# Another order for the last gate/up tile's products in a two-FFN decoder step, new homes for four split weights, and a closing with priority

## The chip, the core and the metric

The kernel runs on one core of a Trainium2 chip. A core has a matrix engine (TensorE, "PE" in the profile; its weight loads are listed apart as "PEld"), a vector engine (VectorE, "DVE"), an activation engine (ScalarE, "ACT"), a general engine (GpSimd, "POOL") and a queue engine (SyncE, "SP") that only issues DMAs here. Each engine works through its own list of instructions, and semaphores tie the lists together. The metric is the device time of the program in microseconds, lower is better. The three runs of the kernel before took 1035.49, 1036.48 and 1035.54 us: median 1035.54.

## What is computed

One step of a hybrid decoder over 520 token columns (512 of a prompt and 8 single new tokens), model width 1024. The trunk is a half-step SwiGLU FFN, a mixer (pooling heads, and a state-space scan, beside each other), a second half-step FFN and a last normalisation:

```
def _swiglu(x, wg, wu, wd):
    return (jax.nn.silu(x @ wg) * (x @ wu)) @ wd
...
h = h + 0.5 * _swiglu(_rms_norm(h, ffn1_norm[l]), ffn1_w_gate[l], ffn1_w_up[l], ffn1_w_down[l])
m, p, c, s = _hybrid_mixer(_rms_norm(h, mix_norm[l]), ...)
h = h + m
h = h + 0.5 * _swiglu(_rms_norm(h, ffn2_norm[l]), ffn2_w_gate[l], ffn2_w_up[l], ffn2_w_down[l])
...
return _rms_norm(h, final_norm), ...
```

The FFN width is 2816. All data are float32. The change touches the ends of the two FFNs only.

## The kernel before

**Numbers in two parts.** A float32 operand is split into a high part (a cast to the reduced float32 that TensorE takes, on ACT) and a low part (the value less its high part, on DVE). A product of two such operands is three matmuls (`mm3`: high by high, high by low, low by high). `split` does this for a weight that lies in a raw buffer, `load_unit` loads the raw weight first.

**Gate and up by seven products.** The columns are held as two halves of 260. The FFN's 22 tiles of 128 rows need gate times x and up times x for both halves, and this is done in a Strassen-like scheme: instead of eight block products a tile takes seven, numbered 1 to 7, each of four `mm3`, 12 matmuls. `Ffn.load(f)` loads a tile's gate and up weights and makes four split pairs of them: `d1` (for products 1 and 2), `e1` (7 and 5), `e2` (6 and 3) and `d2` (4). `d1` and `d2` live in `wp`, tags `whi` and `wlo`, three buffers each; `e1` and `e2` live in the FFN's own pool `wx`, tags `shi` and `slo`, two buffers each. In the trace these are called by tile and letter: `whi_21a` is d1 of tile 21, `whi_21b` is d2, `shi_21c` is e1, `shi_21d` is e2.

`Ffn.product(f, p)` adds up into one of three accumulators in PSUM: products 1, 6, 7 and 4 one after another into `A`; 2 into the first half of `BE`; 5 and 3 into its second half. After 1, 6 and 7 ACT copies what `A` holds (`keep`), so the next product into `A` has to wait for the copy. `gates(f)` makes the gate from the finished `BE` and the copies. `close(f)` takes what product 4 leaves in `A`, multiplies it with the gate on DVE, and splits the result `g` (high part on ACT, low part on DVE). `step(f)` runs one tile: product 1, then product 4 and the closing of the tile before, then 5, 6, 3, 7, 2 and `gates`.

**Down.** `rest` runs the tiles in three chunks of 8, 8 and 6, and after each multiplies the chunk's `g` with the down weights. For each of eight output blocks d there is one unit of weights. In the last chunk a unit is 128 by 768: six k-steps, one for each tile, and the last of them needs `g` of tile 21. In FFN 1 the last chunk goes through `down`, with units from `load_unit`. In FFN 2 it goes through `down_by_half`, which does all eight blocks for the first half of the columns and then for the second. It begins with the first five k-steps of blocks 0 to 2 (15 matmuls each), which do not need tile 21. There, units 0 to 2 come from `load_unit`, into the three `whi`/`wlo` buffers; units 3 to 7 are split into `dhi` and `dlo` in the pool `hg` (called `wd` there), which is opened where the transformed input `xt` (tiles `xth`, `xtl`) lay. Every product reads `xt`, product 4 of tile 21 last, so nothing is written to `dhi` or `dlo` before that. Raw down weights come in pairs of buffers: units 0 and 1, 2 and 3, 4 and 5, 6 and 7 share a pair each, there are two pairs, and a pair is loaded again when both its units are split.

`done(d, b)` scales a finished block on DVE (`th`, line 406), adds it to `h` (line 407) and hands it on. The accumulators of `down_by_half` are the same PSUM banks: `BE` for blocks 0, 1, 4, 5 and `A` for 2, 3, 6, 7. A block can only start when the earlier one in its bank has been taken out by line 406.

**The order.** Tile lays out each engine's list when the kernel is built: it takes whatever its own simulated timeline says is ready, by priority, which normally is the order of the program. `tc.high_priority()` puts a block's instructions ahead of others that are ready. An engine's list is fixed from then on.

Of the kernel before, what the change touches and what calls it, by code (L numbers as in the profile page):

```python
# [10 lines left out]
F32R = mybir.dt.float32r  # L11
# [5 lines left out]
P = 128  # L17
# [6 lines left out]
KD = D // P  # L24
FFN = 2816
KF = FFN // P
# [35 lines left out]
def tile_trunk_step(ctx: ExitStack, tc: tile.TileContext, ins: dict, outs: dict):  # L62
# [7 lines left out]
    wp = ctx.enter_context(tc.tile_pool(name="wp", bufs=3, side="right"))  # L70
# [24 lines left out]
    def raw_tile(name):  # L95
        if not half:
            t = raw_pair(name)
            half.extend([t[:, 1], t[:, 0]])
        return half.pop()

    def split(src, n, name, hp, nb, tags):
        hi, lo = (hp.tile([P, 1024], F32R, tag=t, bufs=nb, name=f"{t}_{name}")[:, :n] for t in tags)
        h, l = hi, lo
        if len(src.shape) == 3:
            h, l = (t.rearrange("p (j c) -> p j c", j=src.shape[1]) for t in (hi, lo))
        nc.scalar.copy(h, src)  # L106
        nc.vector.tensor_tensor(out=l, in0=src, in1=h.bitcast(F32), op=ALU.subtract)
        return hi, lo

    def load_unit(src, n, name):  # L110
        raw = raw_tile(name)[:, :n]
        nc.sync.dma_start(out=raw, in_=src)
        return split(raw, n, name, wp, 3, ("whi", "wlo"))

    def mm3(ps, whi, wlo, xhi, xlo, start, stop, **kw):
        nc.tensor.matmul(ps, whi, xhi, start=start, stop=False, **kw)  # L116
        nc.tensor.matmul(ps, whi, xlo, start=False, stop=False, **kw)  # L117
        nc.tensor.matmul(ps, wlo, xhi, start=False, stop=stop, **kw)  # L118

    def ws(w, k, m=P):  # L120
        return w[:, k * m : (k + 1) * m]
# [73 lines left out]
    class Ffn:  # L195
# [111 lines left out]
        def rest(self, before, last_chunk):  # L307
            lo = 0
            for c, n in enumerate(CHUNKS):
                hi = lo + n  # L310
                last = hi == KF
                for f in range(self.direct if c == 0 else lo + 1, hi if last else hi + 1):
                    self.step(f)
                if last:
                    self.product(KF - 1, 4)
                    self.close(KF - 1)
                    wd = before()
                else:
                    self.product(hi + 1, 1)
                    self.product(hi, 4)  # L320
                    self.close(hi)
                if last and wd is not None:
                    self.down_by_half(c, lo, last_chunk, wd)
                else:
                    self.down(c, lo, hi, last_chunk if last else None)
                lo = hi

        def step(self, f):
            if f not in self.A:
                self.product(f, 1)  # L330
            if f - 1 not in self.g and f > self.direct:
                self.product(f - 1, 4)
                self.close(f - 1)
            for p in (5, 6, 3, 7, 2):
                self.product(f, p)
            self.gates(f)

# [39 lines left out]
        def down_by_half(self, c, lo, after, wd):  # L377
            n = KF - lo
            banks, units = {}, []
            for d in range(KD):  # L380
                src, name = ins[f"w{self.i}d"][d, :, lo * P :], f"{self.i}d{d}_{c}"
                if d < 3:
                    units.append(load_unit(src, n * P, name))
                    continue
                raw = raw_tile(name)[:, : n * P]
                nc.sync.dma_start(out=raw, in_=src)
                hi, lw = (wd.tile([P, n * P], F32R, tag=t, bufs=KD - 3, name=f"{t}_{name}") for t in ("dhi", "dlo"))
                nc.scalar.copy(hi, raw)
                nc.vector.tensor_tensor(out=lw, in0=raw, in1=hi.bitcast(F32), op=ALU.subtract)
                units.append((hi, lw))  # L390

            def part(d, b, ks):
                if (d, b) not in banks and d % 4 < 2:
                    t = ps[0].tile([P, 2, 512], F32, tag="BE", bufs=2, name=f"dh{self.i}_{d}{b}")
                    banks[d, b], banks[d + 1, b] = t[:, 0], t[:, 1]
                elif (d, b) not in banks:
                    banks[d, b] = ps[0].tile([P, 512], F32, tag="A", bufs=2, name=f"dh{self.i}_{d}{b}")
                wh, wl = units[d]
                for k in ks:
                    g = self.g[lo + k]  # L400
                    mm3(banks[d, b][:, :HB], ws(wh, k), ws(wl, k), g[:, 0, b], g[:, 1, b], k == 0, k == n - 1)

            def done(d, b):
                hs = HALVES[b]
                t = self.wx.tile([P, 2, HB], F32, tag="tg", bufs=2, name=f"th{self.i}_{d}{b}")[:, 0]
                nc.vector.tensor_tensor(out=t, in0=banks[d, b][:, :HB], in1=self.rn[:, hs], op=ALU.mult)
                nc.vector.tensor_tensor(out=h[:, d, hs], in0=t, in1=h[:, d, hs], op=ALU.add)
                after(d, b, hs)

            for d in range(3):  # L410
                part(d, 0, range(n - 1))
            for b in range(2):
                for d in range(KD):
                    part(d, b, range(n - 1, n) if b == 0 and d < 3 else range(n))
                    done(d, b)
# [629 lines left out]
```

## Time and profile before

| what | us |
|---|---|
| median of three runs | 1035.54 |
| the profiled execution, its own time | 1034.07 |
| its span (first to last instruction) | 1032.3 |
| PE busy in the span | 983.7 |
| end of FFN 1: last matmul of product 4 of tile 21 starts at | 338.49 |
| first matmul of the mixer starts at | 370.99 |
| end of FFN 2: last matmul of product 4 of tile 21 starts at | 980.34 |
| last down matmul of FFN 2 starts at | 1016.78 |

In the rows below, times are microseconds from the start of the span. A row of the timeline has start, duration, engine, line of the kernel, operation, output and inputs, shape and count; in brackets stands how long the engine had been idle before it and which instruction released it. "SPq" is the issue of a DMA. A matmul's shown duration (0.28) is longer than the distance from one start to the next (0.12), since they are pipelined: the distance is what it costs.

### The profile page before, as it was taken

How to read it: one execution, taken by the hardware profiler on the slowest of the kernel's cores; microseconds unless marked ns; L12 is line 12 of the kernel's file. 1: busy time of each engine (PE TensorE's matmuls, PEld its weight loads, DVE VectorE, ACT ScalarE, POOL GpSimd, SP SyncE). 2: the span in 40 equal slices, each digit the busy share in tenths (PEclk: the TensorE clock that was granted, in tenths of full speed). 3: DMA queues.
4: the chain of work that ended last, by engine and by line, in shares of the span. 5: the costliest groups of instructions: out<-in, count | busy, mean ns of one | idle time of the engine just before them, and what ended most of it. 6: DMA issues, size and time to landing. Idle time of an engine off the chain costs nothing.

```text
span 1032.3 us, 19314 instructions
## 1 busy us (share of the span) xinstructions
PE 983.7 (95%) x7848; PEld 958.9 (93%) x7848; DVE 809.1 (78%) x1403; ACT 526.4 (51%) x884; POOL 57.8 (6%) x109
## 2 busy tenths in 40 slices
PE   7999999999999999997798999999999999999984
PEld 6999999999999999997688999899999999999983
DVE  6999557995578787789989877999945899458766
ACT  7566314663145546775585435566622566225452
POOL 0000000000000001338211000000000000000000
PEclk9999999999999999998899999999999999999997
DMA  5333223232231233345444222223223232332213
GB/s 181 115 123 123 83 90 115 83 123 82 96 110 62 89 134 131 130 155 188 127 157 152 95 86 82 83 83 123 83 95 110 83 122 83 99 107 83 92 32 83
DMA packets 45352, 110.25 MB, mean 107 GB/s; under 512 B 5896, under 2 KB 17096, under 8 KB 45264
## 3 DMA queue, kind: packets, MB, share of 16 engines
q1 hardware_dynamic: 45264, 109.03, 31.9%
q8 instruction: 61, 1.00, 0.4%
q14 instruction: 27, 0.22, 0.1%
HBM read 101.67 MB, written 7.34 MB: 106 GB/s over the span
## 4 chain that ended last, share of the span: by engine, by line
PE 80%; DVE 9%; ACT 6%; issue 2%; DMA 2%; SPq 0%; DVEq 0%; ACTq 0%
PE A L116 7%; PE A L117 7%; PE A L118 7%; PE dn L118 7%; PE dn L116 7%; PE dn L117 7%; PE BE L116 6%; PE BE L118 5%; PE BE L117 5%; PE P L228 3%; PE wo L116 2%; PE wo L118 2%; PE wo L117 2%; PE inz L116 1%; PE inz L117 1%
## 5 line engine op out<-in xcount | busy, mean ns | idle before, releaser
L355 DVE TENSOR_TENSOR td<-dn,rn 128x520 f32<-128x520 f32 x40 | 27.9, 699 | 113.2 <-PE dn L118 113.2
L116 PE MATMUL dn<-g,whi_1d 128*128 128x260 f32 x352 | 99.5, 283 | 1.7 <-ACT whi_1d L106 1.5
L117 PE MATMUL dn<-g,whi_1d 128*128 128x260 f32 x352 | 99.3, 282 | 0.0
L118 PE MATMUL dn<-g,wlo_1d 128*128 128x260 f32 x352 | 99.2, 283 | 0.0
L116 PE MATMUL dn<-g,whi_2d 128*128 128x260 f32 x256 | 72.5, 283 | 1.6 <-ACT whi_2d L106 1.6
L117 PE MATMUL dn<-g,whi_2d 128*128 128x260 f32 x256 | 72.4, 283 | 0.0
L118 PE MATMUL dn<-g,wlo_2d 128*128 128x260 f32 x256 | 72.3, 284 | 0.0
L116 PEld LDWEIGHTS dn<-g,whi_1d 128*128 128x128 f32 x352 | 66.2, 188 | 2.4 <-ACT whi_1d L106 2.0
L117 PEld LDWEIGHTS dn<-g,whi_1d 128*128 128x128 f32 x352 | 66.3, 188 | 0.0
L118 PEld LDWEIGHTS dn<-g,wlo_1d 128*128 128x128 f32 x352 | 66.2, 188 | 0.0
L284 ACT COPY ac<-A 128x260 f32<-128x260 f32 x123 | 45.9, 373 | 37.7 <-PE A L118 36.1
L106 ACT CAST whi_1d<-raw_1d 128x1024 fp32r<-128x1024 f32 (+1 forms) x24 | 23.4, 979 | 73.0 <-PE dn L117 63.0
L106 ACT CAST whi_2d<-raw_2d 128x1024 fp32r<-128x1024 f32 (+1 forms) x19 | 19.3, 1018 | 68.4 <-PE dn L117 59.3
L228 PE MATMUL P<-xg_f,raw 128*128 128x260 f32 x192 | 45.9, 397 | 5.7 <-DMA raw<-in_w1gu 5.7
L116 PEld LDWEIGHTS dn<-g,whi_2d 128*128 128x128 f32 x256 | 48.4, 189 | 2.0 <-ACT whi_2d L106 2.0
L256 DVE TENSOR_TENSOR s<-raw 128x1024 f32<-128x1024 f32 x41 | 50.0, 1219 | 0.0
L117 PEld LDWEIGHTS dn<-g,whi_2d 128*128 128x128 f32 x256 | 48.3, 189 | 0.0
L228 PEld LDWEIGHTS P<-xg_f,raw 128*128 128x128 f32 x192 | 37.4, 199 | 11.6 <-ACT sq_f L154 5.7
L118 PEld LDWEIGHTS dn<-g,wlo_2d 128*128 128x128 f32 x256 | 48.1, 189 | 0.0
L116 PE MATMUL inz<-xh_mx,whi_inz 128*128 128x260 f32 x128 | 37.7, 294 | 0.0
L116 PE MATMUL wo<-catg,whi_wo 128*128 128x260 f32 x128 | 37.5, 293 | 0.2 <-DVE h L869 0.2
L116 PE MATMUL inx<-xh_mx,whi_inx 128*128 128x260 f32 x128 | 37.4, 292 | 0.0
(1326 smaller groups left out, 3933.9 us busy)
## 6 DMA issues: line engine op xcount, KB each, us to landing
raw<-in_w2gu SPq DMA_DIRECT2D x44, 512.0 KB, 3.8
raw<-in_w1gu SPq DMA_DIRECT2D x42, 512.0 KB, 4.4
raw_1d<-in_w1d SPq DMA_DIRECT2D x16, 512.0 KB, 3.9
raw_2d<-in_w2d SPq DMA_DIRECT2D x16, 512.0 KB, 4.1
raw_wo<-in_w_out SPq DMA_DIRECT2D x12, 512.0 KB, 4.7
h<-in_state_ssm SPq DMA_DIRECT2D x16, 256.0 KB, 4.4
ab<-scr_acs SPq DMA_DIRECT2D x8, 512.0 KB, 5.1
out_nss<-h SPq DMA_DIRECT2D x16, 256.0 KB, 3.0
```

The source lines that it names most:

```text
L106: nc.scalar.copy(h, src)
L116: nc.tensor.matmul(ps, whi, xhi, start=start, stop=False, **kw)
L117: nc.tensor.matmul(ps, whi, xlo, start=False, stop=False, **kw)
L118: nc.tensor.matmul(ps, wlo, xhi, start=False, stop=stop, **kw)
L228: nc.tensor.matmul(self.banks[f, u][b][:, :HB], ws(self.raw[f][:, u], j + 4 * q), xg[:, slot[q]], start=j == q == 0, stop=j == 3 and q == ...
L256: nc.vector.tensor_tensor(out=s1, in0=diag, in1=up0, op=ALU.add)
L284: nc.scalar.copy(keep, out[:, :HB])
L355: nc.vector.tensor_tensor(out=t, in0=banks[d][:, :, :HB], in1=self.rn.rearrange("p (b t) -> p b t", b=2), op=ALU.mult)
```

## The change

Three edits. In `rest`, the closing of the last tile gets priority, in both FFNs. In `step`, the last tile takes its products in the order 2, 5, 6, 3, 7 rather than 5, 6, 3, 7, 2, in both FFNs. In `down_by_half` (FFN 2), units 2 and 3 are now split into the `shi`/`slo` buffers that e1 and e2 of the tile leave; units 0 and 1 stay in `whi`/`wlo`, and 4 to 7 stay in the pool `hg`, with four buffers each rather than five. All units now go through `split` or the same two lines as before, with the DMA issued ahead of it.

```diff
                 if last:
                     self.product(KF - 1, 4)
-                    self.close(KF - 1)
+                    with tc.high_priority():
+                        self.close(KF - 1)
                     wd = before()
...
-            for p in (5, 6, 3, 7, 2):
+            for p in (2, 5, 6, 3, 7) if f == KF - 1 else (5, 6, 3, 7, 2):
                 self.product(f, p)
             self.gates(f)
...
             for d in range(KD):
                 src, name = ins[f"w{self.i}d"][d, :, lo * P :], f"{self.i}d{d}_{c}"
-                if d < 3:
-                    units.append(load_unit(src, n * P, name))
-                    continue
                 raw = raw_tile(name)[:, : n * P]
                 nc.sync.dma_start(out=raw, in_=src)
-                hi, lw = (wd.tile([P, n * P], F32R, tag=t, bufs=KD - 3, name=f"{t}_{name}") for t in ("dhi", "dlo"))
+                if d < 4:
+                    home = (wp, 3, ("whi", "wlo")) if d < 2 else (self.wx, 2, ("shi", "slo"))
+                    units.append(split(raw, n * P, name, *home))
+                    continue
+                hi, lw = (wd.tile([P, n * P], F32R, tag=t, bufs=KD - 4, name=f"{t}_{name}") for t in ("dhi", "dlo"))
                 nc.scalar.copy(hi, raw)
                 nc.vector.tensor_tensor(out=lw, in0=raw, in1=hi.bitcast(F32), op=ALU.subtract)
                 units.append((hi, lw))
```

## The prediction

> **What bounds the kernel now.** I read the page first, then PE's waits, then the two stretches that the change touches, FFN 1's end (312 to 376 us) and FFN 2's end (960 to 1033 us), engine by engine.
>
> ```profile
> span 1032.3 us, 19314 instructions
> PE 983.7 (95%) x7848; PEld 958.9 (93%) x7848; DVE 809.1 (78%) x1403; ACT 526.4 (51%) x884; POOL 57.8 (6%) x109
> ...
> PE 80%; DVE 9%; ACT 6%; issue 2%; DMA 2%; SPq 0%; DVEq 0%; ACTq 0%
> ```
>
> PE's list sets the time: 95% busy, and 80% of the chain that ended last. The change adds and removes no matmul, so it can only win or lose stops of PE. Its waits in FFN 2's last stretch (960 to 1033 us), as total, times, longest:
>
> ```profile
> PE psl L523 <- DVE acc_last L147: 2.9, 1, 2.9
> PE dh L116 <- DVE th L406: 2.7, 3, 1.5
> PE dh L116 <- ACT whi_2d L106: 0.8, 1, 0.8
> ```
>
> The first belongs to the last normalisation, behind the last down matmul, and stays. The other two are in what is edited (of the three times in the second row, two are shown below with 1.52 and 0.52; the third, 0.7, is at 1012, in the finish of the first half of the columns, and stays too). PE's own timeline shows what they cost:
>
> ```profile
> 979.04 0.28 PE L116 MATMUL A<-xth_f,whi_21b 128*128 128x260 f32 x1
> ...
> 980.34 0.28 PE L118 MATMUL A<-xth_f,wlo_21b 128*128 128x260 f32 x1
> 981.42 0.39 PE L116 MATMUL dh<-g,whi_2d 128*128 128x260 f32 x1 [0.80 <-ACT whi_2d L106]
> 981.65 0.28 PE L117 MATMUL dh<-g,whi_2d 128*128 128x260 f32 x1
> 982.16 0.38 PE L116 MATMUL dh<-g,dhi_2d 128*128 128x260 f32 x1 [0.23 <-ACT dhi_2d L388]
> 982.38 0.28 PE L117 MATMUL dh<-g,dhi_2d 128*128 128x260 f32 x1
> 982.50 0.31 PE L118 MATMUL dh<-g,wlo_2d 128*128 128x260 f32 x1
> ...
> 988.77 0.28 PE L118 MATMUL dh<-g,dlo_2d 128*128 128x260 f32 x1
> 990.57 0.39 PE L116 MATMUL dh<-g,whi_2d 128*128 128x260 f32 x1 [1.52 <-DVE th L406]
> ...
> 991.72 0.39 PE L116 MATMUL dh<-g,whi_2d 128*128 128x260 f32 x1 [0.52 <-DVE th L406]
> 991.94 0.28 PE L117 MATMUL dh<-g,whi_2d 128*128 128x260 f32 x1
> 992.06 0.28 PE L118 MATMUL dh<-g,wlo_2d 128*128 128x260 f32 x1
> ```
>
> Product 4 of tile 21 is 12 matmuls with eleven steps from 979.04 to 980.34, 0.12 us each. That is the price of a matmul here. Stop 1: from 980.34 to 982.50 there are five steps, 0.60 us of work in 2.16, so 1.56 us are lost. Stop 2: from 988.77 to 992.06 there are six steps (990.57, .79, .92, 991.72, .94, 992.06), 0.72 us in 3.29, so 2.57 us are lost. Together **4.13 us**. Why, the chain of waits tells, in order of time:
>
> ```profile
> 980.54 0.84 ACT whi_2d L106
> ...
> 982.28 0.96 DVE dlo_2d L389
> ...
> 983.26 0.33 SPq L386
> ...
> 983.63 4.70 DMA raw_2d<-in_w2d
> ...
> 988.35 0.84 ACT dhi_2d L388
> ...
> 989.21 0.96 DVE dlo_2d L389
> 990.17 0.35 DVE th L406
> ```
>
> Product 4 ends; only then may unit 2 be split (its `whi` was d2's) and unit 3 (its `dhi` lies where `xt` lay). Stop 1 is PE waiting for these. When unit 3's low part is made, its raw pair is free, SP issues the loads of units 6 and 7, the second lands 4.70 us later, unit 7 is split, and only then DVE comes to the first `th`, which stood behind that split in its list. Stop 2 is PE waiting for that `th` to empty a bank. Both stops hang on one event, the splits of units 2 and 3 after product 4.
>
> **The change, part by part.**
>
> *The new homes.* Unit 2 and unit 3 now want the buffers of e1 and e2 of tile 21: e2 is done with product 3, e1 with product 7, both ahead of product 4. The work is the same (one cast of 0.84, one subtraction of 0.96 each), only earlier. Stop 1 goes, unless what comes after product 4 is too little to cover the closing (below). The loads of 6 and 7 go out when unit 3 is split. Product 7 ends a little before 977 (next part); with the copy of `A`, the cast, the subtraction that is 979.2 or so, against 983.26. With 0.37 for the issue, 4.70 to land, 0.84 and 0.96 unit 7 is whole near 986, and the first `th` right behind it. The bank that it empties is wanted by block 6, when PE is through the six blocks before it: 108 matmuls, some 40 of them ahead of product 4, so 68 x 0.12 = 8.2 us after it, near 990. Four us of slack: stop 2 goes. Moved DMAs: the loads of 4 and 5, 6 and 7, on a SP queue that carries nothing else from there to the output:
>
> ```profile
> 967.04 17.73 SPq L386 DMA_DIRECT2D raw_2d<-in_w2d  x5
> 1008.87 18.09 SPq L534 DMA_DIRECT2D out_y<-hg  x8
> ```
>
> Value: -4.13; bounds -4.13 and -1.56 (rival A).
>
> *The order of products.* The same 12 matmuls stand earlier, cost nothing in themselves, and free d1 one tile-product earlier for unit 1. But product 2 used to stand between 6 and 7, or 7 and 4, while ACT copies `A`. The list keeps such successors far apart:
>
> ```profile
> 971.22 0.28 PE L118 MATMUL A<-xth_f,slo_21d 128*128 128x260 f32 x1
> ...
> 974.22 0.28 PE L116 MATMUL A<-xth_f,shi_21c 128*128 128x260 f32 x1
> ...
> 975.54 0.29 PE L118 MATMUL A<-xth_f,slo_21c 128*128 128x260 f32 x1
> ```
>
> From 6's last to 7's first it is 3.0 us, from 7's last to 4's first (979.04) 3.5 us, though the copy after 7 is done early:
>
> ```profile
> 976.25 0.36 ACT L284 COPY ac<-A 128x260 f32<-128x260 f32 x1
> ```
>
> Between 7 and 4 it puts down matmuls that need no tile 21. The rows by line count them before product 4 (each of the three lines of `mm3` has ten, 30 in all):
>
> ```profile
> L116 PE MATMUL dh<-g,whi_2d x10: 278/282/287, 974.0 to 978.7; 128*128 128x260 f32 x10
> ```
>
> With product 2 gone forward, only 3 (12 matmuls, 1.4 us) is left for the distance between 6 and 7, and some 10 more down matmuls will fill it: product 4 ends 1.2 us later with 40 down matmuls done instead of 30. PE is busy all the while, so by itself this costs 0. If nothing were put there, PE would have the copy to wait for, 0.94 us after 7's last began (976.25 + 0.36 against 975.54, less a step), 1.0 us at most in each FFN: bound +2.0.
>
> *The cover for the closing.* What PE has after product 4 that needs no `g` of tile 21: blocks 0 to 3, five k-steps, 4 x 15 = 60, now that unit 3 is split early; less 40 is 20 matmuls, 2.4 us. What the closing takes, before:
>
> ```profile
> 338.49 0.29 PE L118 MATMUL A<-xth_f,wlo_21b 128*128 128x260 f32 x1
> 339.43 0.62 ACT L299 CAST g<-tg 128x520 fp32r<-128x520 f32 x1
> 340.43 0.69 DVE L300 TENSOR_TENSOR g<-tg,g 128x520 fp32r<-128x520 f32 x1
> 983.48 0.62 ACT L299 CAST g<-tg 128x520 fp32r<-128x520 f32 x1
> 984.88 0.70 DVE L300 TENSOR_TENSOR g<-tg,g 128x520 fp32r<-128x520 f32 x1
> ```
>
> In FFN 1 the last part of `g` is ready at 341.12, 2.6 us after product 4's last began; in FFN 2 at 985.58, 5.2 us, for four casts stood ahead of it on ACT and four subtractions on DVE. With priority these can't go first once `g`'s own is ready; one may slip in while DVE makes the product with the gate, as in FFN 1. I take FFN 1's 2.6 us for both: against 2.4 + 0.12 of cover, 0.1 to 0.3 us of a stop. What the priority pushes back on ACT and DVE are the splits of units 4 to 7, wanted when PE gets to block 4, 20 + 12 matmuls after product 4 (3.8 us); unit 4 needs 0.84 + 0.96 and the closing's 1.4 in between. That fits. Value +0.2; bounds 0 and +2.6 (no cover left).
>
> *FFN 1.* Units 0 and 1 have 60 such matmuls too, less 40 is 20: the same 2.4 us. Its one stop in the edited stretch is for a bank, not for `g`:
>
> ```profile
> 343.53 0.28 PE L118 MATMUL dn<-g,wlo_1d 128*128 128x260 f32 x1
> 344.00 0.39 PE L116 MATMUL dn<-g,whi_1d 128*128 128x260 f32 x1 [0.19 <-DVE td L355]
> ```
>
> From there to 370 us PE has no stop; the busy times (the first pair is the stretch and PE) show it, and DVE with 23.98 of 26 us:
>
> ```profile
> 344.00:370.00 26.00, 26.00 (x216) 25.89 (x216) 23.98 (x53) 15.37 (x34) 0.42 (x1) 1.00 0.31 96
> ```
>
> Unit 2's split there waits for product 4 as before and is now behind the closing, some 1 us later, but its first matmul is the one at 344.00, 3 us after. Value 0; bounds -0.35 (that stop) and +2.6 (no cover).
>
> **Sum.** -4.13 + 0.2 + 0 = -3.9 us. The profiled execution took 1034.07 (span 1032.3 and 1.8 around it), which becomes 1030.2. The median of the runs is 1.5 above it, so on their scale 1035.54 - 3.9 = **1031.6**. If the mechanism works, its own range is 1030.8 to 1033.2.
>
> **The rivals.** A. *Only stop 1 goes.* Unit 3's cast is late, behind the closing that now has priority: product 4 ends near 981.7, the cast and subtraction near 983.5, the loads land near 988.6, unit 7 is whole near 990.4, and if the list keeps the first `th` behind it, PE wanting the bank from 990 waits for 2 us all told. For it: in the list of before `th` stands behind unit 7's split, and a list can't be changed at run time. The Trainium skill (TensorE: Matmul & The Clock Gate, under Architectural detail) says the same of the engine, that VectorE takes its queue strictly in order; the chain above agrees, with `th` at 990.17 right after the subtraction at 989.21. Against it: product 7 frees the home some 4 us before product 4 ends, and ACT is idle from 976.61 to 980.54. Price: gain 1.9, time 1033.6. Chance 0.15.
>
> B. *It doesn't do what it says*: the list leaves the splits of 2 and 3 behind product 4 though their homes are free. Then the stops stay, 1035.5. Against it: unit 0 and 1 were split as soon as theirs were free. Chance 0.06.
>
> C. *The cover is spent* (slower). The place is PE's list between product 7 and the closing, in both FFNs: the builder, now with four ready units, puts nearly all 60 down matmuls ahead of product 4. Then PE stands for the whole closing. Each matmul above some 38 ahead of product 4 costs 0.12 in each FFN, 0.24 together; the 4.13 is eaten from 38 + 17 = 55 on. With all 60 in front it is 2 x 2.6 = 5.2 us against 4.13, and up to 2.6 more if FFN 2's closing stays as slow as it is now (5.2): 1036.6 to 1039.2. For it: the distances of 3.0 and 3.5 us are the builder's own, and the new order gives it less to put between. Against: the two distances need some 40 matmuls, not 55. Chance 0.16.
>
> D. *Another order further on.* All lists after tile 21 of FFN 1 are laid out anew, with DVE nearly full from 344 to 370, and the mixer behind it. For a price I take the first of those PE stops either way, 1 to 3 us on top of the forecast: 1028.6 to 1034.6. For: any shift of DVE's order there falls on a list with 2 us to spare in 26. Against: FFN 1 ends at PE's own pace in both. Chance 0.11, half of each sign.
>
> **The numbers.** The forecast has 0.52. About 0.2%, 2.1 us, is what a measurement of this kernel can tell from no change: faster is below 1033.5, slower above 1037.6. Faster: 0.52, half of A's 0.15 and most of D, 0.09: 0.69. Same: half of A, B, the slower end of D and 0.06 of C: 0.21. Slower: the rest of C: 0.10. The range runs from D's better part to C's lower part, 1029.3 to 1036.8; outside are most of C and D's ends, some 0.17.
>
> **What would show it.** Stop 1 right: no gap in PE's list after product 4 of tile 21 above 0.3 us, and `shi_2d` casts ahead of product 4's end. Stop 2 right: the last two loads of down weights issued near 979 rather than 983.26, the first `th` near 986, no gap before block 6. The order: some 40 down matmuls ahead of product 4, whose end moves to about 981.7. The closing: 2.6 us in both FFNs. FFN 1: the first mixer matmul within 0.5 us of 370.99. The forecast is wrong if the loads of 6 and 7 still go out after product 4, if a new gap opens between 7 and 4 or before the first matmul on tile 21, or if the mixer's length changes.

## The result, and the profile after

The changed kernel is faster. The four first runs have a median of 1030.51 us against 1036.0 of the kernel before, a ratio of 0.9948 with a 95% interval of 0.993 to 0.9965. Timed twice more, in the experiments below, it gave 0.996 (0.9946 to 0.9974) and 0.9972 (0.9961 to 0.9983). So the gain is 3 to 5 us; its profiled execution took 1030.91 us against 1034.07, 3.2 less. Its page:

```profile
span 1029.1 us, 19313 instructions
PE 981.7 (95%) x7848; PEld 956.6 (93%) x7848; DVE 807.3 (78%) x1403; ACT 526.4 (51%) x884; POOL 57.0 (6%) x109
```

PE's waits from 955 us on in the changed kernel (who waits for what, the total in us, how often, the longest):

```profile
PE psl L525 <- DVE acc_last L147: 2.9, 1, 2.9
PE dh L116 <- DVE th L408: 1.2, 2, 0.7
```

The waits on `whi` and `dhi` are gone, that on `th` has shrunk from 2.7 to 1.2 us. The timeline of PE in the changed kernel at the two places where it stopped before (start, length, then the instruction; in brackets the wait ahead of it):

```profile
980.72 0.28 PE L118 MATMUL A<-xth_f,wlo_21b 128*128 128x260 f32 x1
980.83 0.28 PE L118 MATMUL dh<-g,slo_2d 128*128 128x260 f32 x1
...
987.74 0.28 PE L118 MATMUL dh<-g,wlo_2d 128*128 128x260 f32 x1
988.54 0.39 PE L116 MATMUL dh<-g,whi_2d 128*128 128x260 f32 x1 [0.52 <-DVE th L408]
988.76 0.28 PE L117 MATMUL dh<-g,whi_2d 128*128 128x260 f32 x1
...
990.69 0.28 PE L118 MATMUL dh<-g,wlo_2d 128*128 128x260 f32 x1
990.81 0.28 PE L116 MATMUL dh<-g,dhi_2d 128*128 128x260 f32 x1
```

Product 4 ends and the next matmul starts 0.11 us later, with unit 2 in its new home (`slo`). Stop 1 (1.56 us) is gone. Stop 2 is 0.78 us (988.76 less 987.74, less two steps of 0.12) where it was 2.57.

Which matmul waits there? From 988.54 to 990.69 stand 18 in a row on `whi_2d` and `wlo_2d`. In the changed kernel these hold units 0 and 1 only, and both have had their 36 matmuls of the first half by 987.74. So PE goes from block 4 straight to block 0 of the second half, ahead of blocks 5 to 7, and not to block 6, as the prediction has it. (The rows show that it is block 0 or 1; by the order of the program it is 0.) That block takes the pair of banks which blocks 0 and 1 leave, so it waits for the `th` of block 1, whose last matmul is the one at 987.74. The rows of before, in the prediction, can be read in the same way: stop 2 was two waits. First 1.79 us were lost up to 990.92, in the three matmuls of a block's last k-step (by its bank, block 1's), behind the first `th`; then 0.78 us up to 991.94, ahead of block 0 of the second half. The new homes took the first away, all but 0.07 us, and left the second as it was.

What feeds stop 2, from the same kernel's timeline of SP, ACT and DVE, in order of time (for SP the length runs over the x issues of one line):

```profile
972.81 7.04 SPq L384 DMA_DIRECT2D raw_2d<-in_w2d  x4
...
975.65 0.84 ACT L106 CAST shi_2d<-raw_2d 128x768 fp32r<-128x768 f32 x1 [2.39 <-PE BE L117]
977.10 0.83 ACT L106 CAST shi_2d<-raw_2d 128x768 fp32r<-128x768 f32 x1 [0.61 <-PE A L117]
...
980.91 1.57 ACT L390 CAST dhi_2d<-raw_2d 128x768 fp32r<-128x768 f32 x2 [2.17 <-PE A L117]
982.39 0.62 ACT L299 CAST g<-tg 128x520 fp32r<-128x520 f32 x1
...
983.53 0.69 DVE L300 TENSOR_TENSOR g<-tg,g 128x520 fp32r<-128x520 f32 x1
984.14 1.82 DVE L391 TENSOR_TENSOR dlo_2d<-raw_2d,dhi_2d 128x768 fp32r<-128x768 f32 x2
986.91 0.43 DVE L408 TENSOR_TENSOR th<-dh,rn 128x260 f32<-128x260 f32 x1 [0.96 <-PE dh L118]
```

Units 2 and 3 are split as products 3 and 7 let go of their homes, 5 and 4 us before product 4 ends. The last two loads are out by 979.85 instead of 983.6 and later. DVE is through with unit 7 at 985.96 and then stands idle 0.96 us: the first `th` now waits for PE, not PE for DVE's list.

To compare kernels whose mixers differ from one execution to the next (last section), I use two lengths from PE's timeline: **stage 1** from the tenth-last matmul of product 1 of tile 21 in FFN 2 to the first sum of squares (`psl`), and **stage 2** from there to the second `psl`. All times in us:

| kernel | stage 1 | stage 2 | ratio of the runs (95% interval) |
|---|---|---|---|
| before | 965.57 to 1005.46: 39.89 | 14.49 | |
| changed | 965.69 to 1002.32: 36.63 | 14.53 | 0.9948 (0.993 to 0.9965) |
| changed, e1 | 963.64 to 1000.27: 36.63 | 14.54 | 0.996 (0.9946 to 0.9974) |
| changed, e9 | 966.70 to 1003.30: 36.60 | 14.54 | 0.9972 (0.9961 to 0.9983) |
| e2 homes alone | 964.06 to 1000.69: 36.63 | 14.54 | 0.9967 (0.9954 to 0.998) |
| e3 order alone | 966.67 to 1006.67: 40.00 | 14.54 | 1.0001 (0.999 to 1.0011) |
| e4 priority alone | 962.75 to 1002.59: 39.84 | 14.54 | 0.9996 (0.9986 to 1.0006) |
| e5 unit 3 late | 964.86 to 1004.46: 39.60 | 14.52 | 0.9981 (0.9968 to 0.9994) |
| e11 unit 3 late, again | 965.45 to 1003.32: 37.87 | 14.54 | one run |
| e6 closing really first | 967.99 to 1004.53: 36.54 | 14.48 | 0.9967 (0.9953 to 0.998) |
| e7 and last steps first | 967.07 to 1003.07: 36.00 | 13.30 | 0.9955 (0.9941 to 0.997) |
| e8 and finish later | 965.49 to 1001.49: 36.00 | 12.85 | 0.9953 (0.9937 to 0.9968) |
| e10, as e8 | 965.94 to 1001.93: 35.99 | 12.86 | 0.9956 (0.9942 to 0.997) |

The change is worth 3.26 us in stage 1 and nothing in stage 2. At the end of FFN 1 the first mixer matmul starts at 370.76 (370.99 before), 0.1 us earlier when the 0.15 by which the first down matmul (111.17 against 111.32) was ahead already is taken off.

### The profile page after: what moved, and what is told of

Its sections match the earlier page's. It is cut to its first block, busy times and chain, and to the rows that moved or that the text cites. A ratio compares the mean times of both kernels' runs of the same rounds, so it can differ in the third digit from the quotient of the medians.

```text
span 1029.1 us, 19313 instructions
## 1 busy us (share of the span) xinstructions
PE 981.7 (95%) x7848; PEld 956.6 (93%) x7848; DVE 807.3 (78%) x1403; ACT 526.4 (51%) x884; POOL 57.0 (6%) x109
## 4 chain that ended last, share of the span: by engine, by line
PE 42%; DVE 7%; ACT 4%; DMA 2%; issue 1%; POOL 1%; DVEq 0%; ACTq 0%; SPq 0%
PE A L116 4%; PE A L117 4%; PE A L118 4%; PE dn L118 3%; PE dn L116 3%; PE dn L117 3%; PE BE L116 3%; PE BE L118 3%; PE BE L117 3%; PE wo L116 2%; PE wo L118 2%; PE wo L117 2%; PE P L228 1%; PE dh L116 1%; DMA bcb<-scr_bc 1%
## 5 line engine op out<-in xcount | busy, mean ns | idle before, releaser
L118 PE MATMUL inz<-xh_mx,wlo_inz 128*128 128x260 f32 x128 | 36.9, 288 | 0.0
```

## The experiments

Four kernels (e2 to e5) take the change apart, two (e6, e7) ask what is left of stop 2 and why, and one (e8) builds on the answer. e1, e9, e10 and e11 run a kernel again.

**e1, the changed kernel again.**

> The changed kernel once more, timed in five rounds. Theory T (the whole gain is the two stops at the end of FFN 2, -3.3 us there in the profile, nothing elsewhere): ratio 0.9969, 0.996 to 0.998. Rival R (the first timing's 0.9948 is real, 2 us more come from an earlier stage, such as the mixer): ratio 0.994 to 0.9955, and a profile with a mixer some 2 us shorter.

0.996, at the edge of T's range; the 0.9969 that the profile's 3.3 us would give lies within its interval, and so does R's 0.9955. Stage 1 is 36.63 us to the last digit. The third timing, e9, is 0.9972, with R's range outside its interval. In the mixer every engine's list is row for row that of the kernel before, so R has no place to gain in; why the first timing came out 2 us lower is not shown, other than that the mixer's length varies by as much between executions of one program.

**e2, the homes alone.** The changed kernel less the other two edits:

```diff
-            for p in (2, 5, 6, 3, 7) if f == KF - 1 else (5, 6, 3, 7, 2):
+            for p in (5, 6, 3, 7, 2):
...
-                    with tc.high_priority():
-                        self.close(KF - 1)
+                    self.close(KF - 1)
```

> Units 2 and 3 in the homes of e1 and e2, but the old order of products and no priority. Theory T (the homes carry it: e2 is free after product 3 and e1 after product 7, in the old order too, 8 and 5 us before product 4 ends): both stops go as in the changed kernel, -2.8 to -3.6 us, the loads of units 6 and 7 near 979. Rival R (the new order is what frees the homes in time): the gain is at most stop 1, -1.6 us, and the loads go out after product 4 as before, near 983.

The timeline of SP in this run, and then PE's waits from 950 us on:

```profile
954.91 21.98 SPq L383 DMA_DIRECT2D raw_2d<-in_w2d  x8
```

```profile
PE dh L116 <- DVE th L407: 1.2, 2, 0.7
```

All eight loads are out by 976.89, 2.1 us before product 4's last matmul (978.96) starts. Stage 1 is 36.63, the same as with all three edits. T holds: the homes are the whole gain of the stage. In the old order too, e2 and e1 are done well before product 4.

**e3, the order alone.** The kernel before, with `(2, 5, 6, 3, 7)` for the last tile.

> Product 2 first in the last tile of both FFNs, units 2 and 3 where they were, no priority. Theory T (12 matmuls moved under a busy PE): -0.5 to +0.5 us, stop 1 (1.6) and stop 2 (2.6) both still there, FFN 1's end within 0.3 us. Rival R (the order matters by itself, through the earlier split of unit 1): at least 1.5 us faster. Rival C of the prediction (fewer matmuls between 6 and 7, so the cover is spent): at least 1 us slower, with a new stop before the first matmul that needs tile 21.

PE's waits from 950 us on in this run:

```profile
PE dh L116 <- DVE th L406: 2.8, 3, 1.6
PE dh L116 <- ACT whi_2d L106: 0.8, 1, 0.8
PE dh L116 <- ACT dhi_2d L388: 0.2, 1, 0.2
```

Both stops are there as before, stage 1 is 40.00 against 39.89, the ratio 1.0001. T holds, and rival C of the prediction has no sign here: 30 down matmuls stand ahead of product 4, as many as before, and no new stop.

**e4, the priority alone.** The kernel before, with the closing under `tc.high_priority()`.

> Priority for the closing of the last tile, nothing else. Every engine's list of instructions is, row for row, that of the kernel before. Theory T (so the priority does nothing at all): no difference, 0.9985 to 1.0015, which is then the scatter of a program against itself; the closing in FFN 2 still ends 5.2 us after product 4's last matmul begins. Rival R (the closing gets ahead, as the prediction had it): 2.6 us there.

The timeline of PE and DVE around the closing in this run:

```profile
977.52 0.28 PE L118 MATMUL A<-xth_f,wlo_21b 128*128 128x260 f32 x1
978.60 0.39 PE L116 MATMUL dh<-g,whi_2d 128*128 128x260 f32 x1 [0.80 <-ACT whi_2d L106]
...
982.06 0.69 DVE L300 TENSOR_TENSOR g<-tg,g 128x520 fp32r<-128x520 f32 x1
```

`g` is ready at 982.75, 5.2 us after product 4's last matmul, as before, and stop 1 is there. The ratio is 0.9996. The lists show why: with or without the priority, all five are the same, row for row, also with the other two edits in place. A likely reason, which is argued and not shown, is that the splits ahead of the closing are ready in the builder's timeline while the closing is still waiting for its own inputs, and a priority only chooses among what is ready. This is also a program against itself: its profiled execution took 1030.26 us, and the one of before 1034.07.

**e5, unit 3 late.** The changed kernel with unit 3 back in the pool:

```diff
-                if d < 4:
+                if d < 3:
...
-bufs=KD - 4
+bufs=KD - 3
```

> The changed kernel with unit 3 back in the pool hg, so split after product 4; unit 2 keeps its new home. It takes the two stops apart. Theory T (stop 1 is the split of units 2 and 3, stop 2 the loads of 6 and 7, which go out when unit 3 is split): PE has only 28 - 15 = 13 matmuls after product 4 that it can do at once, so stop 1 is 0 to 0.5 us; the last load goes out about 2 us after product 4 and stop 2 is back with 1 to 2.6 us. Gain 1.5 to 2.5 us of 3.3. Rival R (stop 2 is only the order of DVE's list, not the late loads): stop 2 stays at 0.8, gain 3.

Product 4's last matmul starts at 979.89 and the next at 980.00: no stop 1. The last two loads go out from 982.06 on, and stop 2 is back: PE goes from 986.66 to 989.37 in six steps, 2.71 us, so 2.0 us are lost (0.72 of work). So far T, and R falls: DVE's list now has the first `th` behind unit 6's split (986.25) and the second behind unit 7's (987.47), and these wait for the late loads. But stage 1 is 39.60, nearly as long as before. The rest is in what comes after the stop. The windows of this run (length, PE busy, weight loads, DVE, ACT, POOL, then PE's granted clock):

```profile
986.66:989.37 2.71, 1.15 (x7) 0.72 (x6) 2.71 (x7) 1.10 (x3) 0.00 (x0) 1.00 0.00 0
989.37:992.89 3.52, 3.52 (x19) 3.52 (x19) 3.31 (x11) 3.18 (x9) 0.00 (x0) 0.53 0.00 0
```

and the same run's timeline of PE:

```profile
987.60 0.39 PE L116 MATMUL dh<-g,whi_2d 128*128 128x260 f32 x1 [0.66 <-DVE th L408]
...
989.15 0.39 PE L116 MATMUL dh<-g,whi_2d 128*128 128x260 f32 x1 [0.91 <-DVE th L408]
...
990.29 0.42 PE L116 MATMUL dh<-g,whi_2d 128*128 128x260 f32 x1
990.50 0.42 PE L117 MATMUL dh<-g,whi_2d 128*128 128x260 f32 x1
```

For 3.5 us the clock stands at 0.53 and a matmul costs 0.22 instead of 0.12: 16 to 17 of them, 1.5 us lost. e11 runs the same kernel once more.

> One more look at the kernel with unit 3 split late, whose profile showed PE at a clock of 0.53 for 3.5 us after its two stops. If the drop belongs to this pattern of stops, it is there again and the stretch from tile 21 to the first half's end is near 39.6 us; if it hangs on where a window of the clock's control falls, it is gone and the stretch is near 38.1 us.

The windows of this run at the same two places:

```profile
987.25:989.82 2.57, 1.13 (x7) 0.71 (x6) 2.57 (x7) 0.96 (x3) 0.00 (x0) 1.00 0.00 0
989.82:993.34 3.52, 3.52 (x31) 3.52 (x31) 3.31 (x11) 3.18 (x9) 0.00 (x0) 1.00 0.00 0
```

The stops are alike (2.57 us for the same six steps, 1.85 lost) and the clock stays at 1.00; stage 1 is 37.87, 2.0 less than before. So unit 2's new home alone is worth 2.0 us (stop 1, which was 1.56, and a part of stop 2), and unit 3's, with the earlier loads, the other 1.2 (37.87 less 36.63). Whether the clock falls differed between two executions of one program. The five rounds of e5 gave 0.9981, 2 us.

**e6, the closing really first.** From here on the base is the homes alone. The splits of units 5 to 7 are tied behind the closing's two, on their engines:

```diff
-            nc.scalar.copy(g[:, 0], tg)
-            nc.vector.tensor_tensor(out=g[:, 1], ...)
+            hi = nc.scalar.copy(g[:, 0], tg)
+            lo = nc.vector.tensor_tensor(out=g[:, 1], ...)
+            self.closed = hi.ins, lo.ins
...
+                with ExitStack() as st:
+                    for i in self.closed if d > 4 else ():
+                        st.enter_context(tc.issue_after(i))
                     nc.scalar.copy(hi, raw)
                     nc.vector.tensor_tensor(out=lw, ...)
```

> Homes alone, and the splits of units 5 to 7 tied behind the closing's two on ACT and DVE (what the priority was for). Theory T (after product 4 PE still has some 29 matmuls, 3.5 us, that need no tile 21): g is ready 2.7 us after product 4 rather than 3.5 to 4.4, and the stop before block 6 shrinks by 0 to 0.8 as block 0's last step comes earlier; -3.3 to -4.0 us against before. Rival R (the closing bounds this stage, as the prediction's cover counted): PE's matmuls there end 1 us or more earlier than in homes alone.

The timeline of DVE in this run, at the closing and at the first `th`:

```profile
984.83 0.69 DVE L300 TENSOR_TENSOR g<-tg,g 128x520 fp32r<-128x520 f32 x1
...
988.62 0.43 DVE L411 TENSOR_TENSOR th<-dh,rn 128x260 f32<-128x260 f32 x1 [0.49 <-PE dh L118]
```

`g` is ready at 985.52, 2.6 us after product 4's last matmul (982.89), and it buys 0.09 us in stage 1. The stop ahead of the second half is unchanged: the step is 0.80 us, as in the changed kernel. T's lower end; R falls: the closing was covered.

**e7, and the last steps first.** On top of e6, PE does the last k-step of blocks 0 to 3 ahead of block 4:

```diff
-            for d in range(3):
+            for d in range(4):
                 part(d, 0, range(n - 1))
+            for d in range(4):
+                end = part(d, 0, range(n - 1, n))
             for b in range(2):
                 for d in range(KD):
-                    part(d, b, range(n - 1, n) if b == 0 and d < 3 else range(n))
+                    if b or d > 3:
+                        with tc.issue_after(end.ins) if b == 0 and d == 4 else nullcontext():
+                            part(d, b, range(n))
                     done(d, b)
```

> As the run before it, and on PE the last k-step of blocks 0 to 3 ahead of block 4. Theory T (what is left of stop 2, 0.78 us, is PE's list, which does blocks 0 to 4 side by side and so empties the first bank late): the first th starts some 1.5 us earlier, the stop is gone, 0.8 us less than homes alone from tile 21 to the first half's end (36.63 becomes 35.8). Rival R (DVE's list is what is late): the stop stays.

The timeline of DVE and PE in this run, at the first two `th` and where PE goes on from block 4 to block 0 of the second half:

```profile
987.13 0.76 DVE L412 TENSOR_TENSOR th<-dh,rn 128x260 f32<-128x260 f32 x2
...
989.04 0.28 PE L118 MATMUL dh<-g,dlo_2d 128*128 128x260 f32 x1
989.16 0.28 PE L116 MATMUL dh<-g,whi_2d 128*128 128x260 f32 x1
```

No stop: the step is 0.12. Stage 1 falls to 36.00, 0.63 less than with the homes alone; T holds, though the first `th` comes 1.15 us earlier after product 4 than with the homes alone, not 1.5, and R falls. What was not expected is stage 2, 13.30 instead of 14.54: a stop of PE in the second half, 0.87 us long, is gone too. The first `psl` now stands three matmuls later in PE's list, which moves 0.36 us from stage 2 to stage 1; the two stages together are 1.7 us shorter than in e6, about what the two stops cost. Blocks are now finished one after another there rather than side by side; that this is what took the second stop away was not tested apart.

**e8, and the finish later.** On top of e7, the scaling of the first half's output on DVE is held behind the `th` of block 3 of the second half (`finish(0)` is cut after its square root, and the reciprocals and products follow at block 3 under `tc.issue_after`).

> As the run before it, and the scaling of the first half's output (two reciprocals, four products on DVE) held behind the th of block 3 of the second half. Theory T (the 0.87 us stop of PE in the second half is DVE at that scaling while a bank waits): the stop goes, 0.9 us less again, the ratio to before near 0.995. Rival R (the scaling then delays later th, or the output's DMAs end the kernel): no gain, 0 to +1 us.

PE's waits from 950 us on in this run:

```profile
PE psl L536 <- DVE acc_last L147: 2.5, 1, 2.5
```

The stop it was made for had gone with e7, so the expected 0.9 is not there. Stage 2 is 0.45 shorter, with a shorter wait ahead of the second `psl` (2.5 against 2.9).

**e9 and e10, the changed kernel and that version on one chip.**

> The changed kernel beside the version of the run after it, on one chip. By the profiles it is 3.2 us below before: ratio 0.997, and 2.3 us above that version.

> The version with the homes alone, the closing really first, the last steps first and the later finish, again. By its profile's stage (54.4 us before, 51.2 in the changed kernel, 48.9 here, from tile 21 to the second sum of squares) ratio 0.9945 to 0.9955 to before, and 0.9978 to the changed kernel. Rival: no difference from the changed kernel that these runs can show.

0.9972 (0.9961 to 0.9983) and 0.9956 (0.9942 to 0.997). The intervals overlap (0.9961 to 0.997), so the runs alone do not tell the two kernels apart; the two stages together are 51.14 and 48.85 us, and were the same to 0.05 us in each kernel's profiles. That version, the homes alone with e6 to e8, is by these stages the fastest of all, 5.5 us below before; by its timings it is 4.6 and 4.9 us below.

## Why the prediction was right, point by point

- **What bounds, and both stops on one event: right.** Taking the splits of units 2 and 3 out from behind product 4 (e2, no other edit) gives the whole gain, and putting unit 3 back (e5, e11) brings the late loads and a larger stop 2 back, not stop 1. One part of stop 2 hung on something else, as follows.
- **The new homes, -4.13: the mechanism right, the size too large by 0.78.** Stop 1 went wholly. Of stop 2 the forecast was that the first `th` would follow unit 7's split near 986, with 4 us to spare for block 6. The split was done at 985.96, but the first `th` came at 986.91, since PE had not finished block 0: its list does blocks 0 to 4 side by side. The term counted 108 matmuls ahead of block 6 as if they finished block by block; PE's list has 90 of them (blocks 0 to 4) and then block 0 of the second half, which wants its bank 0.12 us after block 1's last matmul. So the second of stop 2's two waits, 0.78 us before and after, never hung on the splits, and the prediction took it for a part of the same event. e7 bears this out: with the last steps of blocks 0 to 3 ahead of block 4 the wait is gone.
- **The order of products, 0: right, for another reason.** No cost and no gain (e3). The forecast of some 40 down matmuls ahead of product 4 was off: there are 32 (12 before product 3, 20 after product 7), and product 4 ends within 0.4 us of where it did. The list puts 12 between 6 and 3 and fewer after 7 (20 rather than 28). The order is not needed for the homes either (e2).
- **The closing, +0.2: the end right, the way wrong.** The prediction expected 2.6 us in both FFNs, by the priority. It does nothing: the lists are the same with and without it (e4), and FFN 1's closing takes its 2.6 us before and after. The closing takes 3.5 us in the changed kernel (984.22 less 980.72), shorter than 5.2 only because two casts rather than four stand ahead of it. It cost nothing since the cover was longer than counted: not 20 but 39 matmuls stand between product 4 and the first that needs tile 21 (985.52), 28 of blocks 2 and 3 and 11 of block 4, 4.8 us. `g` is ready 1.3 us before that, and e6, which really gets it to 2.6, gains 0.09.
- **FFN 1, 0: right.** 0.1 us, with the same stop for a bank.
- **Sum.** Forecast -3.9, measured -3.26 in the stage, -2.9 to -5.4 by the three timings. 1031.6 was predicted; the medians of the three timings are 1030.51, 1029.54 and 1031.99, beside 1036.0, 1033.75 and 1034.56 for the kernel before. Some of the closeness is luck: the first timing lies 2 us below what the stage explains, and the 0.2 for the closing took back a little of the 0.78 too much.
- **The rivals.** A (stop 2 stays): its time is that of e5 and e11, which split unit 3 where A feared it; in the changed kernel ACT did it at 977.10, right after product 7. The Trainium skill's rule on VectorE's queue (TensorE: Matmul & The Clock Gate, Architectural detail) held, with the first `th` at 986.91 behind the split that ended at 985.96, but that split was done in time. B and C did not come about. D (another order further on) neither: the mixer's length differs between runs of one program by as much as was feared, and not by order: from the end of FFN 1 to tile 21 of FFN 2 every engine's list is row for row that of before.

## What to carry to other kernels

When several stops follow one another, look for the event that they hang on, and check each wait against it: here two stops, 8 us apart, came mostly from buffers that were free too late, and homes that were free 4 to 5 us earlier removed 3.3 of 4.1 us; the rest was a wait of its own. Read from the weights which block a waiting matmul belongs to. The priority changed nothing here; compare the lists before explaining what one did, and use an explicit edge where the order matters. Blocks that are finished side by side all empty their banks late: where the next block waits for a bank, finish one first.

## What the runs showed of the hardware

**PE's clock fell after short stops in one execution and not in another of the same program.** e5 and e11 are one program with stops alike: in one the clock went to 0.53 for 3.5 us (1.5 us lost), in the other it stayed at 1.00. In the kernel before, 1.79 and 0.78 us lost at the same place did not lower it either.

**In the mixer it falls too, but at the place compared here what is lost is given back.** For each of the next two kernels stand PE's longest wait between 460 and 480 us (as total, times, longest) and then the window from 465 to 480 us (columns as above, with the share of the DMA engines and GB/s behind the clock). The kernel before, its waits:

```profile
PE yd L835 <- DVE ab L820: 3.1, 1, 3.1
```

and its window:

```profile
465.00:480.00 15.00, 11.87 (x84) 10.71 (x84) 15.00 (x39) 8.29 (x19) 11.28 (x15) 0.81 0.43 151
```

e4, the same program, its waits:

```profile
PE yd L836 <- DVE ab L821: 1.5, 1, 1.5
```

and its window:

```profile
465.00:480.00 15.00, 13.46 (x115) 12.47 (x114) 15.00 (x43) 6.76 (x15) 10.57 (x15) 1.00 0.41 131
```

A wait of 1.5 us leaves the clock at 1.00; with 3.1 us it is 0.81 over the window, and 84 matmuls get done instead of 115. Over all thirteen profiles, this wait is 1.5 to 2.4 us in four and 2.6 us in the changed kernel, all with a clock of 1.00; it is 2.5 us in e9 (0.89), and 2.8 to 3.8 us in the other seven (0.80 to 0.89). What it costs in the end shows where PE next stands for DVE, by its timeline in the kernel before

```profile
493.97 1.19 PE L832 MATMUL pst<-xw,bt 128*128 128x512 f32 x1 [6.66 <-DVE E L846]
```

and in e4:

```profile
492.13 2.04 PE L833 MATMUL pst<-xw,bt 128*128 128x512 f32 x2 [6.83 <-DVE E L847]
```

The first matmul behind the wait starts at 475.19 in the kernel before and at 473.34 in e4, 1.85 us apart; the same matmul further on, under the lower clock, at 480.94 and 476.51, 4.43 apart; `pst` at 493.97 and 492.13, 1.84 apart. PE stands for DVE there in either, so the fall of the clock cost nothing beyond that point, and the longer wait for DVE did. In the same comparison e11, whose clock falls here, is 0.03 us earlier than e5, then 2.74 later, then again 0.03 earlier. So at this place the scatter is that of the wait and not of the clock; places further on in the mixer were not compared. A difference of 3 us between single profiles of this kernel says nothing until the stages are compared. What makes that wait itself vary, between 1.5 and 3.1 us for the same lists, was not tried.

The Trainium skill (TensorE: Matmul & The Clock Gate, Why this matters for your kernels) asks for no gaps above some 3 us between bursts of matmuls, and says (What's actually happening) that the activity is judged over a window of about 3.4 us that runs freely. The mixer's rows agree with the first to within half a microsecond: from 2.8 us on the clock always fell, up to 2.4 us never, and in e9 it fell at 2.5. e5 goes below it: two stops of 0.93 and 1.17 us lost, with matmuls between them, were enough once, and once not, which fits a window that starts anywhere.
